# Expert weights loaded in rows of 16 KB, with the other tenants of the store packed into few pages

## The chip, the cores and the metric

The kernel runs on one core of one Trainium2 chip. The metric is the device time of one execution, in microseconds (us); lower is better. The kernel before takes 1248.84 us, the median of three executions (1247.45 to 1250.5).

## The reference, cut to what matters

One encoder layer on 512 tokens of width 1024, all in float32: token mixing with eight latent-attention heads and four differential-attention heads, then a mixture of 16 SwiGLU experts, each of which takes the 64 tokens with the highest affinity for it. Of the bytes that the layer reads, the three weight arrays of the experts are nearly all: 16 x 1024 x 2048, twice, and 16 x 2048 x 1024, in float32, which is 384 MiB.

```python
def reference(x, c, positions, ...):
    c_act = jax.nn.silu(c)
    mod = jnp.einsum('bd,dn->bn', c_act, w_ada[l]) + b_ada[l]
    sh_a, sc_a, g_a, sh_f, sc_f, g_f = jnp.split(mod[:, None, :], 6, axis=-1)
    u = x * (1.0 + sc_a) + sh_a
    mix = attention_mixer(u, positions, rel_bias, w_in[l], ..., w_out[l], l)
    x = layer_norm(DEEPNORM_ALPHA * x + g_a * mix, ln1_g[l], ln1_b[l])
    u = x * (1.0 + sc_f) + sh_f
    ffn = expert_choice_ffn(u, w_router[l], w_gate[l], w_up[l], w_down[l])
    return layer_norm(DEEPNORM_ALPHA * x + g_f * ffn, ln2_g[l], ln2_b[l])

def expert_choice_ffn(u, w_router, w_gate, w_up, w_down):
    cap = CAPACITY_FACTOR * S // N_EXPERTS                      # 64
    aff = jax.nn.softmax(jnp.einsum('bsd,de->bse', u, w_router), axis=-1)
    g, idx = lax.top_k(jnp.swapaxes(aff, 1, 2), cap)
    xs = jax.vmap(lambda ub, ib: ub[ib])(u, idx)
    h = jax.nn.silu(jnp.einsum('becd,edf->becf', xs, w_gate)) * jnp.einsum('becd,edf->becf', xs, w_up)
    y = jnp.einsum('becf,efd->becd', h, w_down) * g[..., None]
    ...                                                         # the rows of y are added back to their tokens
```

## The kernel before

**Stages.** In a first stage the modulation vector (products of `wadaT` with c, on DVE) and the first input projection (`w_a`, on PE) are made while their weights arrive: for each of eight blocks, two loads of `wadaT` (L207, L208), one of `xT` (L253) and one of `w_a` (L254). Behind it, in the same queue, come a table for the position bias, written by one DMA from `f_d` to `bias_d` in DRAM and read back (L481, L532), and the weights of the second projection, `w_q` (L326). Then come 32 attention steps, s = 0 to 31, whose extra work is put at a step by `at(...)`; the mixed heads are kept as `MX`, the rows of `w_out` are loaded by `wo_load` and split in two parts by `wo_split`, and the four blocks of x itself, for the residual sum, are loaded by `x_load` (L788). Up to here the list scheduler of the language sets the order of the instructions on each engine. From `crit` on the order is that of the code: output projection, layer norm, router, top-64 by `DVE.max`, and then the experts.

**Experts.** They go in eight pairs, pr = 0 to 7, and the two experts of a pair share the 128 rows of the array (64 tokens each). `gather` makes the transposed tokens `xs` by matmuls with a one-hot matrix, a scale `Gc` and a shift `Bc` per column of the model width. `up` multiplies them with `w_gate`, then with `w_up`, in eight steps k of 128 model rows; `hidden_t` transposes the product; `down` multiplies with `w_down` in eight steps b of 256 rows. `scatter` adds the result to the tokens, one pair later.

**The store.** 24 pages of 8 KB per partition (`Pages`) hold everything large: the weights and the data of the attention, and later the expert weights. `get` returns a free page, or a part of one, with the one that has been free longest first; `put` gives it back. The list `stream` has every load of expert weights in the order of use; each is 1 MiB, 8 KB in each of 128 partitions, and fills a page. `prefetch` issues loads from it, in SP's queue, for as long as a page is free:

```python
            for k in range(KB):
                for e in range(2):
                    off = w.offset + ((2 * pr + e) * D + k * P) * FF
                    stream.append(((pr, nm, k, e), bass.AP(tensor=w.tensor, offset=off, ap=[[FF, P], [1, FF]])))
...
    def prefetch(keep=0):
        while stream and pages.free() > keep:
```

It is called once at step 29 of the attention (with 3 pages kept), once ahead of `crit` (with 2 kept), once ahead of the top-64, and then in `turn`, which gives back the two pages of a step k or b when its matmuls have been written down. A load into a page that was given back waits, in SP's queue, for the last matmul that reads it. The matmuls on the weights of `up` are L1365, those of `down` and most others go through the helper `mm` (L121), and the transposes of `hidden_t` are L1396, those of the router L948.

## Time and profile before

| what | value |
|---|---|
| median of three executions | 1248.84 us |
| the profiled execution | 1253.39 us |
| its span in the trace | 1251.6 us |
| PE busy | 1173.6 us (94%) |
| DVE busy | 373.0 us (30%) |
| ACT busy | 229.6 us (18%) |
| POOL busy | 34.0 us (3%) |
| moved by DMA | 456.03 MB, mean 364 GB/s |
| mean granted clock of TensorE | 0.986 |

The span runs from the first to the last record of the profiled execution, and 1.8 us of its time lie around it. The span is cut into 40 slices of 31.3 us where the page gives a rate in slices. The busy shares are means over stages that differ: the first 320 us are the attention and the router, the rest are the experts. PE's time of a matmul record is modelled to its end, and its weight loads (PEld) overlap with it. A row of a group gives the line, the engine, the operation, its tiles and shapes, the count; then the busy time and the mean time of one in ns; then the idle time ahead of it and what ended most of it.

### The profile page before, as it was taken

The numbers are of one execution on the slowest core, as the hardware profiler recorded it, in microseconds if no ns is written. First come the engines' busy times: TensorE is split into PE (matmuls) and PEld (weight loads), VectorE is DVE, ScalarE is ACT, GpSimd is POOL, SyncE is SP. The second block draws the span as 40 slices with busy tenths as digits, with TensorE's granted clock in tenths as the row PEclk, the third lists the DMA queues.
The fourth block names the chain that finished last, engine by engine and source line by source line (L and its number), as shares of the span: only waits on it lengthen the run. The fifth ranks groups of instructions, "written<-read, shape, count | busy, mean of one in ns | idle before, by whom it ended". The sixth has DMA issues, their size and how long they took to land.

```text
span 1251.6 us, 14038 instructions
## 1 busy us (share of the span) xinstructions
PE 1173.6 (94%) x5657; PEld 554.1 (44%) x5657; DVE 373.0 (30%) x827; ACT 229.6 (18%) x473; POOL 34.0 (3%) x31
## 2 busy tenths in 40 slices
PE   8999999998999999999998899789979997999897
PEld 4877677775434333433432243234323432433232
DVE  6868889866001111111020102011101110111016
ACT  3555885433010000000000000000000000001001
POOL 0000000000000410000000000000000000000003
PEclk8999999998999899999999999999999999999998
DMA  9872426588999999999999999999999999999993
GB/s 335 314 269 90 164 99 211 175 338 344 366 420 422 420 390 422 422 420 421 421 422 421 420 421 422 421 420 422 422 420 421 422 422 421 420 422 421 421 401 130
DMA packets 76360, 456.03 MB, mean 364 GB/s; under 512 B 8285, under 2 KB 8669, under 8 KB 28163
## 3 DMA queue, kind: packets, MB, share of 16 engines
q1 hardware_dynamic: 76002, 455.02, 89.8%
q8 instruction: 44, 0.72, 0.2%
q14 instruction: 24, 0.19, 0.0%
q10 hardware_dynamic: 290, 0.10, 0.0%
HBM read 452.98 MB, written 3.95 MB: 365 GB/s over the span
## 4 chain that ended last, share of the span: by engine, by line
DMA 43%; PE 31%; DVE 1%; issue 0%; POOL 0%; ACT 0%; POOLq 0%; SPq 0%; DVEq 0%; ACTq 0%
DMA pg<-in_w_up_dram 17%; PE bk L121 17%; DMA pg<-in_w_down_dram 14%; PE bk L1365 13%; DMA pg<-in_w_gate_dram 11%; PE bk L1242 1%; POOL pg L1494 0%; PE bk L1396 0%; DVE lst L1476 0%; PE bk L1289 0%; POOLq L1623 0%; PE bk L1314 0%; DVE mv L1477 0%; DVE pg L1433 0%; ACT aff L879 0%
## 5 line engine op out<-in xcount | busy, mean ns | idle before, releaser
L1365 PE MATMUL bk<-pg,xs 128*64 128x512 f32 x2048 | 475.8, 602 | 49.2 <-DMA pg<-in_w_up_dram 47.6
L121 PE MATMUL bk<-pg,pg 128*64 128x512 f32 (+3 forms) x2138 | 466.2, 479 | 11.8 <-ACT pg L136 3.7
L121 PEld LDWEIGHTS bk<-pg,pg 128*64 128x64 f32 (+1 forms) x2138 | 236.9, 158 | 191.1 <-issue 130.6
L1365 PEld LDWEIGHTS bk<-pg,xs 128*64 128x64 f32 x2048 | 146.7, 137 | 350.4 <-issue 247.9
L1390 DVE TENSOR_TENSOR pg<-pg,bk 128x512 f32<-128x512 f32 x32 | 22.0, 687 | 338.4 <-PE bk L1365 310.1
L143 ACT ACTIVATE pg<-bk 128x512 f32<-128x512 f32 (+1 forms) x97 | 55.0, 582 | 352.0 <-PE bk L1396 318.2
L1300 DVE TENSOR_TENSOR pg<-pg,bk 128x512 f32<-128x512 f32 x56 | 38.5, 687 | 125.8 <-PE bk L121 125.4
L1283 DVE TENSOR_SCALAR xs<-bk,Gc,Bc 128x128 f32<-128x128 f32 x32 | 13.1, 410 | 207.9 <-PE bk L121 207.9
L121 PEld LDWEIGHTS bk<-ohg,pg 128*128 128x128 f32 x512 | 59.7, 191 | 27.3 <-issue 27.3
L121 PE MATMUL bk<-ohg,pg 128*128 128x128 f32 x512 | 66.0, 282 | 0.5 <-DVE ohg L1271 0.5
L121 PE MATMUL bk<-pg,ohg 128*128 128x512 f32 x120 | 59.2, 617 | 0.2 <-DVE pg L1433 0.2
L1281 ACT ACTIVATE xs<-bk,Bc,Gc 128x128 f32<-128x128 f32 x32 | 14.6, 457 | 201.3 <-PE bk L121 201.3
L143 ACT ACTIVATE ohg<-bk 128x512 f32<-128x512 f32 x8 | 4.8, 597 | 241.9 <-PE bk L1289 241.9
L136 ACT ACTIVATE pg<-pg 128x512 fp32r<-128x512 f32 (+2 forms) x63 | 42.7, 708 | 33.5 <-DMA pg<-in_w_q_dram 10.0
L1049 DVE CUSTOM_DVE_ANT_0 pg<-pg,pg 128x1024 f32<-128x1024 f32 x32 | 38.7, 1219 | 3.1 <-DMA pg<-in_wadaT_dram 3.1
L121 PEld LDWEIGHTS bk<-pg,ohg 128*128 128x128 f32 x120 | 20.4, 189 | 38.2 <-issue 37.6
L236 DVE TENSOR_TENSOR pg<-pg,pg 128x512 fp32r<-128x512 f32 (+1 forms) x34 | 31.0, 920 | 11.5 <-ACT pg L136 11.4
L1433 DVE SCALAR_TENSOR_TENSOR pg<-bk,lst,pg 128x512 f32<-128x512 f32 x16 | 12.0, 751 | 74.5 <-PE bk L121 73.7
L1386 ACT ACTIVATE pg<-bk 128x512 f32<-128x512 f32 x32 | 18.8, 598 | 60.2 <-PE bk L1365 60.2
L1396 PEld LDWEIGHTS bk<-csb,pg 128*128 128x128 f32 x128 | 17.7, 207 | 26.5 <-DVE pg L1390 13.5
L1450 POOL TENSOR_TENSOR pg<-pg,pg 128x512 f32<-128x512 f32 x4 | 5.1, 1273 | 786.9 <-DMA pg<-in_w_down_dram 782.9
L567 ACT ACTIVATE pg<-pg,st 128x512 f32<-128x512 f32 x32 | 23.0, 720 | 11.8 <-DVE st L563 11.6
(223 smaller groups left out, 594.6 us busy)
## 6 DMA issues: line engine op xcount, KB each, us to landing
pg<-in_w_gate_dram SPq DMA_DIRECT2D x128, 1024.0 KB, 19.8
pg<-in_w_up_dram SPq DMA_DIRECT2D x128, 1024.0 KB, 19.8
pg<-in_w_down_dram SPq DMA_DIRECT2D x120, 1024.0 KB, 19.8
pg<-in_wadaT_dram SPq DMA_DIRECT2D x16, 1024.0 KB, 6.4
pg<-in_wadaT_dram SPq DMA_DIRECT2D x16, 512.0 KB, 8.1
pg<-in_w_down_dram SPq DMA_DIRECT2D x16, 512.0 KB, 11.0
pg<-bias_d SPq DMA_DIRECT2D x16, 256.0 KB, 4.5
pg<-in_w_out_dram SPq DMA_DIRECT2D x8, 512.0 KB, 3.5
```

What stands on the lines that cost most here:

```text
L121: PE.matmul(o, l, r, start=start, stop=stop)
L136: return ACT.activation(dst, src, AF.Copy, scale=scale)
L143: ACT.activation(dst, src, AF.Copy)
L236: lo_eng.tensor_tensor(lo, src, ff(hi), op=OP.subtract)
L567: ACT.activation(pm, pm, AF.Exp, scale=-1.0, bias=nm[:, m:m + 1], accum_out=ss[:, m:m + 1])
L1049: i = DVE.tensor_tensor_reduce(out=w2[:, j], in0=w2[:, j], in1=cs, scale=1.0, scalar=0.0, op0=OP.mult, op1=OP.add, accum_out=modr[:, n:n + 1])
L1281: ACT.activation(xs[:, k, :], src, AF.Identity, scale=Gc[:, k:k + 1], bias=Bc[:, k:k + 1])
L1300: DVE.tensor_add(acc[t][:, c], acc[t][:, c], bank)
L1365: PE.matmul(banks[c][r], xs[:, k, r], w[e][:, c * 512:(c + 1) * 512], start=k == 0, stop=k == 7)
L1386: ACT.activation(EP["HS"][:, c * 512:(c + 1) * 512], banks[c], AF.Silu)
L1390: DVE.tensor_tensor(s, s, U[c], op=OP.mult)
L1396: PE.transpose(G[c % 2][:, i * P:(i + 1) * P], sj[:, i // 2, i % 2, :], ident)
```

## The change

**Rows.** A load of `w_gate` or `w_up` now takes two neighbouring model rows into one partition, so its rows are 16 KB and one load of 2 MiB serves two steps k (`block`). `gather` takes every second column of x to match, and `Gc` and `Bc` are rearranged to match by small matmuls (`GBp`). `w_down` comes with four neighbouring rows to a partition, and `hidden_t` transposes with a step of four. In the last pair `w_down` is loaded by pieces of 8 KB and of two times 2 KB in a row.

**Sheets.** A load of 2 MiB goes into a sheet of 16 KB per partition. The store is opened as 12 pools of two pages; when the top two pages are free, `sheet` closes that pool and opens one sheet in its place, from the other side. The eight lowest pages (`LOW`) stay pages. A sheet is given back after its second step. Where no sheet is to be had, `prefetch` may load the two halves of a block into two low pages, with rows of 8 KB (`begun`); in the first pair's first two projections, `turn` also allows that (`REUSE`).

**The other tenants.** `get` now chooses low pages, or pages 12 to 16 (`MID`), from step 22 on (`LATE`), and at once for what stays long (`stay`). Two of the mixed heads share a page, the last four splits of `w_out` have pages reserved for them (`WOR`), x has pages 0 and 1, which nothing else may use, and the last rows are loaded into the page of the first ones. `prefetch` is called at steps 30 and 31 too, with 4 pages kept.

The core of the diff:

```diff
+LOW = 8
+LATE = 22
+MID = (12, 17)
+REUSE = "gu"
...
+    def __init__(self, tc, ctx, n, low):
+        self.tc, self.ctx, self.low = tc, ctx, low
...
+    def open(self, name, side):
+        pool = self.tc.tile_pool(name=name, bufs=1, side=side).__enter__()
+        self.ctx.callback(lambda: pool._released or pool.release())
+        return pool
...
-        for i, u in enumerate(self.used):
-            if u and self.kind[i] != kind:
+        for i, u in enumerate(self.used[:top]):
+            if i < first or u and self.kind[i] != kind:
                 continue
...
-                key = (age, u == 0) if old else (u == 0, age)
+                high = (0 if i < self.low else i) if stay else (0 if MID[0] <= i < MID[1] else 1 if i < self.low else i)
+                key = (age, u == 0) if old else (high, u == 0, age) if self.late or stay else (u == 0, age)
                 if best is None or key < best[0]:
...
+    def has_sheet(self):
+        n = len(self.used)
+        return any(not u for u, _, _ in self.sheets) or n > self.low and not self.used[n - 1] and not self.used[n - 2]
+    def sheet(self):
+        free = [x for x in self.sheets if not x[0]]
+        if free:
+            x = min(free, key=lambda x: x[1])
+        else:
+            for v in (self.used, self.stamp, self.t, self.kind):
+                del v[-2:]
+            self.pools.pop().release()
+            i = len(self.sheets)
+            x = [0, 0, self.open(f"sheet{i}", bass.Side.RIGHT if hasattr(bass.Side, "RIGHT") else "right")]
+            self.sheets.append(x)
+        i = next(j for j, y in enumerate(self.sheets) if y is x)
+        self.now += 1
+        x[0] = 1
+        return ("sheet", i), x[2].tile([P, 4096], F32, name=f"sh{i}_{self.now}", tag=f"sh{i}", bufs=1)
...
+        self.now += 1
+        if i == "sheet":
+            assert self.sheets[m][0]
+            self.sheets[m][:2] = [0, self.now]
+            return
         assert self.used[i] & m == m
...
-            h, pg = pages.get()
+            h, pg = pages.get(first=0, top=2)
             Zh.append(h)
...
+        for h in range(2):
+            for j in range(2):
+                for i, v in enumerate((Gc, Bc)):
+                    o = 64 + 8 * i + j
+                    mm(bank[64 * h:64 * h + 64, o:o + 7:2], ident[:, j:127 + j:2], v[:, h:h + 7:2], True, True)
+        copy(ACT, GBp.rearrange("p i k -> p (i k)"), bank[:, 64:80])
...
+    def block(w, ex, rows, b, n):
+        return bass.AP(tensor=w.tensor, offset=w.offset + (ex * rows + b * n * P) * (4096 // n), ap=[[4096, P], [1, 4096]])
...
-            for k in range(KB):
+            for k in range(KB // 2):
                 for e in range(2):
-                    off = w.offset + ((2 * pr + e) * D + k * P) * FF
-                    stream.append(((pr, nm, k, e), bass.AP(tensor=w.tensor, offset=off, ap=[[FF, P], [1, FF]])))
...
-                off = w_down.offset + ((2 * pr + e) * FF + b * 2 * P) * D
-                stream.append(((pr, "d", b, e), bass.AP(tensor=w_down.tensor, offset=off, ap=[[2 * D, P], [1, 2 * D]])))
+                    stream.append(((pr, nm, k, e), block(w, 2 * pr + e, D, k, 2)))
+        for b in range(4):
+            if pr < NP - 1:
+                for e in range(2):
+                    stream.append(((pr, "d", b, e), block(w_down, 2 * pr + e, FF, b, 4)))
+            else:
...
-    def prefetch(keep=0):
-        while stream and pages.free() > keep:
-            key, src = stream.pop()
-            n = math.prod(src.shape[1:])
-            h, pg = pages.get(n // 256)
-            SP.dma_start(pg.rearrange("p (j n) -> p j n", j=2) if len(src.shape) == 3 else pg, src)
-            loaded[key] = (h, pg)
+    begun = []
+    def prefetch(keep=0, low=0, spare=None):
+        while stream and (not keep or pages.free() - 2 * (not begun) >= keep):
+            key, src = stream[-1]
+            if not begun and pages.has_sheet() and not (low == 2 and pages.free(LOW)):
+                h, pg = pages.sheet()
+                if isinstance(src, list):
+                    for n, part in enumerate(src):
+                        o = n % 2 * 2048 + n // 2 * 1024
+                        dst = pg[:, o:o + 2048] if len(src) == 2 else pg[:, o:o + 1024].rearrange("p (j n) -> p j n", j=2)
+                        SP.dma_start(dst, part)
+                else:
+                    SP.dma_start(pg, src)
+                loaded[key] = ([[], [h]], [pg[:, :2048], pg[:, 2048:]])
+                stream.pop()
+            elif (begun or low) and pages.free(LOW) > (0 if spare is None or begun else spare + 1):
+                h, pg = pages.get(top=LOW)
+                SP.dma_start(pg, bass.AP(tensor=src.tensor, offset=src.offset + 2048 * len(begun), ap=[[4096, P], [1, 2048]]))
+                begun.append((h, pg))
+                if len(begun) == 2:
+                    loaded[key] = ([[x] for x, _ in begun], [x for _, x in begun])
+                    begun.clear()
+                    stream.pop()
+            else:
+                break
 
...
+    at(27, ga[7], lambda: put_all([MXh[k] for k in range(4, 8)] + [WOh[k] for k in range(4, 8)]),
+       lambda: WOR.extend(pages.get(8, F32R, stay=True) for _ in range(4)), wo_next(0, 1))
...
+        if s == LATE:
+            pages.late = True
         if s in EARLY:
             prefetch(EARLY[s])
+        if s >= 30:
+            prefetch(4)
...
-                mm(src, Z[t][:, k * P:(k + 1) * P], oh[:, t, :], t == 0, t == 3)
+                mm(src, Z[t][:, k // 2 * 256 + k % 2:k // 2 * 256 + 255 + k % 2:2], oh[:, t, :], t == 0, t == 3)
             if k % 2:
-                ACT.activation(xs[:, k, :], src, AF.Identity, scale=Gc[:, k:k + 1], bias=Bc[:, k:k + 1])
+                ACT.activation(xs[:, k, :], src, AF.Identity, scale=GBp[:, 0, k:k + 1], bias=GBp[:, 1, k:k + 1])
             else:
-                DVE.tensor_scalar(xs[:, k, :], src, Gc[:, k:k + 1], Bc[:, k:k + 1], op0=OP.mult, op1=OP.add)
+                DVE.tensor_scalar(xs[:, k, :], src, GBp[:, 0, k:k + 1], GBp[:, 1, k:k + 1], op0=OP.mult, op1=OP.add)
...
+        if pr == 0 and nm in REUSE and k < 6:
+            prefetch(0, 1, 1)
...
+        for k in range(KB):
+            if k % 2 == 0:
+                h, w = zip(*(loaded.pop((pr, nm, k // 2, e)) for e in range(2)))
             between(k)
             for c in range(4):
-                products(k, c, w)
-            turn(pr, nm, k, h)
-        if n < KB:
...
+                products(k, c, [x[k % 2] for x in w])
+                if k >= n:
+                    columns(c)
+            turn(pr, nm, k, h[0][k % 2] + h[1][k % 2])
...
-        sj = EP["HS"][:, c * 512:(c + 1) * 512].rearrange("p (b q j) -> p b j q", b=2, j=2)
+        sj = EP["HS"][:, c * 512:(c + 1) * 512].rearrange("p (q j) -> p j q", j=4)
         for i in range(4):
-            PE.transpose(G[c % 2][:, i * P:(i + 1) * P], sj[:, i // 2, i % 2, :], ident)
+            PE.transpose(G[c % 2][:, i * P:(i + 1) * P], sj[:, i, :], ident)
```

SP's instructions in the first stage, before. In a row stand the line, the transfer and the shape; a tile's name has its page (`pg13`) and then serial numbers, and x2 is two loads in a row. `f_d` is the position bias on its way to the table in DRAM.

```order
L207 DMA pg13_20_182<-in_wadaT_dram 128x1024
L208 DMA pg13_20_182<-in_wadaT_dram 128x1024
L253 DMA pg11_15_139<-in_xT_dram 128x512
L254 DMA pg14_21_185<-in_w_a_dram 128x1024
L469 DMA f_d_74<-pg0_1_78 4x1024
L207 DMA pg17_27_226<-in_wadaT_dram 128x1024
L208 DMA pg17_27_226<-in_wadaT_dram 128x1024
L253 DMA pg14_21_185<-in_xT_dram 128x512
L254 DMA pg18_28_229<-in_w_a_dram 128x1024
L207 DMA pg20_33_269<-in_wadaT_dram 128x1024
```

The four loads of x come 70 rows further down, behind the loads of the table:

```order
L532 ISA
L532 DMA pg14_21_185<-bias_d_75 128x512
L788 DMA pg21_202_3464<-in_x_dram 128x1024 x2
L788 DMA pg7_201_3461<-in_x_dram 128x1024 x2
L210 DMA pg5_229_3649<-in_wadaT_dram 128x2x1024
L766 DMA pg18_223_3601<-in_w_out_dram 128x1024
L766 DMA pg20_232_3665<-in_w_out_dram 128x1024
```

The same place of the first stage, of the change:

```order
L247 DMA pg15_20_215<-in_wadaT_dram 128x1024
L248 DMA pg15_20_215<-in_wadaT_dram 128x1024
L293 DMA pg13_15_172<-in_xT_dram 128x512
L294 DMA pg16_21_218<-in_w_a_dram 128x1024
L828 DMA pg0_203_3497<-in_x_dram 128x1024 x2
L828 DMA pg1_204_3500<-in_x_dram 128x1024 x2
L509 DMA f_d_107<-pg2_1_111 4x1024
L247 DMA pg19_27_259<-in_wadaT_dram 128x1024
L248 DMA pg19_27_259<-in_wadaT_dram 128x1024
L293 DMA pg16_21_218<-in_xT_dram 128x512
L294 DMA pg20_28_262<-in_w_a_dram 128x1024
L247 DMA pg22_33_302<-in_wadaT_dram 128x1024
```

The four loads of x now stand ahead of the write to `f_d`, two blocks of `wadaT` and `w_a`, and all that follows them in the queue.

SP's instructions where the store is filled for the first time and then used again, before (`pg11_364` is a page that the first expert step has given back):

```order
L995 DMA pg6_353_4567<-in_w_gate_dram 128x2048
L995 DMA pg8_354_4569<-in_w_gate_dram 128x2048
L995 DMA pg22_355_4571<-in_w_gate_dram 128x2048
L995 DMA pg20_356_4573<-in_w_up_dram 128x2048
L995 DMA pg23_357_4575<-in_w_up_dram 128x2048
L995 DMA pg2_358_4577<-in_w_up_dram 128x2048
L995 DMA pg14_359_4579<-in_w_up_dram 128x2048
L995 DMA pg0_360_4581<-in_w_up_dram 128x2048
L995 DMA pg13_361_4583<-in_w_up_dram 128x2048
L995 DMA pg11_364_4653<-in_w_up_dram 128x2048
L995 DMA pg1_365_4655<-in_w_up_dram 128x2048
L995 DMA pg12_368_4670<-in_w_up_dram 128x2048
```

The same place of the change (`sh` is a sheet, 4096 elements wide; the page loads are halves):

```order
L1061 DMA sh3_329_4346<-in_w_gate_dram 128x4096
L1066 DMA pg6_351_4618<-in_w_gate_dram 128x2048
L1066 DMA pg4_352_4620<-in_w_gate_dram 128x2048
L1066 DMA pg7_353_4622<-in_w_gate_dram 128x2048
L1061 DMA sh4_354_4628<-in_w_gate_dram 128x4096
L1061 DMA sh5_355_4634<-in_w_up_dram 128x4096
L1061 DMA sh6_356_4640<-in_w_up_dram 128x4096
L1061 DMA sh7_357_4646<-in_w_up_dram 128x4096
L1061 DMA sh0_360_4729<-in_w_up_dram 128x4096
L1061 DMA sh1_361_4731<-in_w_up_dram 128x4096
L1061 DMA sh2_364_4759<-in_w_up_dram 128x4096
L1061 DMA sh3_365_4761<-in_w_up_dram 128x4096
```

Ahead of the first loads into room that the experts give back there were 22 loads of 1 MiB; now there are eight of 2 MiB and six halves, and the room that is given back first is two sheets, where it was two pages.

## Rows read from the trace of the kernel before

**Rows 1.** The page: span, GB/s in 40 slices, instruction queue (packets, MB, share).

```profile
span 1251.6 us, 14038 instructions
...
GB/s 335 314 269 90 164 99 211 175 338 344 366 420 422 420 390 422 422 420 421 421 422 421 420 421 422 421 420 422 422 420 421 422 422 421 420 422 421 421 401 130
...
q8 instruction: 44, 0.72, 0.2%
```

**Rows 2.** Stretches: length, busy us PE, PEld, DVE, ACT, POOL, PEclk, DMA, GB/s.

```profile
280.00:290.00 10.00, 10.00 (x68) 8.07 (x67) 6.99 (x33) 3.04 (x9) 0.00 (x0) 1.00 0.65 252
290.00:300.00 10.00, 5.98 (x56) 3.90 (x55) 7.57 (x33) 5.07 (x13) 0.00 (x0) 0.93 0.84 338
...
310.00:320.00 10.00, 10.00 (x61) 5.36 (x61) 0.82 (x2) 0.91 (x2) 0.00 (x0) 1.00 0.71 279
360.00:600.00 240.00, 239.96 (x1114) 92.11 (x1112) 33.86 (x56) 15.01 (x27) 18.73 (x8) 0.99 1.01 417
600.00:1200.00 600.00, 549.46 (x2472) 207.85 (x2470) 68.62 (x116) 31.76 (x58) 0.00 (x0) 1.00 1.01 421
```

**Rows 3.** PE's costliest group from 600 to 1200 us.

```profile
L1365 PE MATMUL bk<-pg,xs 128*64 128x512 f32 x1280 | 302.8, 601 | 49.2 <-DMA pg<-in_w_up_dram 47.6 <-DMA pg<-in_w_gate_dram 1.6
```

**Rows 4.** DMA issues, 600 to 1200 us: count, KB, median us to landing.

```profile
pg<-in_w_gate_dram SPq DMA_DIRECT2D x80, 1024.0 KB, 19.8
```

**Rows 5.** SP's timeline, 190 to 420 us: start, length, line, transfer, count.

```profile
227.54 0.34 SPq L995 DMA_DIRECT2D pg<-in_w_gate_dram  x1
...
245.96 46.23 SPq L995 DMA_DIRECT2D pg<-in_w_gate_dram  x12
292.24 43.32 SPq L995 DMA_DIRECT2D pg<-in_w_up_dram  x16
```

**Rows 6.** What SP waited for, whole run: us, times, longest.

```profile
SPq L995 <- PE bk L1365: 126.4, 76, 17.0
```

**Rows 7.** DMA packets, 1205 to 1215 us.

```profile
DMA packets 1924, 3.86 MB, mean 386 GB/s; under 512 B 113, under 2 KB 113, under 8 KB 1901
```

**Rows 8.** DMA packets and issues, 20 to 40 us.

```profile
DMA packets 2519, 8.12 MB, mean 406 GB/s; under 512 B 284, under 2 KB 284, under 8 KB 2517
...
pg<-in_wadaT_dram SPq DMA_DIRECT2D x8, 512.0 KB, 9.1
pg<-in_w_a_dram SPq DMA_DIRECT2D x4, 512.0 KB, 8.7
pg<-in_xT_dram SPq DMA_DIRECT2D x4, 256.0 KB, 8.3
```

**Rows 9.** DMA issues of the whole run: the four loads of x.

```profile
pg<-in_x_dram SPq DMA_DIRECT2D x4, 512.0 KB, 3.9
```

**Rows 10.** SP's timeline, 40 to 100 us.

```profile
43.60 0.79 SPq L481 DMA_DIRECT2D bias_d<-f_d  x1
47.14 7.40 SPq L326 DMA_DIRECT2D pg<-in_w_q_dram  x1
...
57.91 2.09 SPq L326 DMA_DIRECT2D pg<-in_w_q_dram  x1
66.58 4.15 SPq L532 DMA_DIRECT2D pg<-bias_d  x6
```

**Rows 11.** What ACT waited for, 40 to 100 us.

```profile
ACT pg L136 <- DMA pg<-in_w_q_dram: 10.0, 5, 5.4
```

**Rows 12.** PE's timeline, 308 to 331 us: the first expert steps.

```profile
312.39 3.65 PE L1365 MATMUL bk<-pg,xs 128*64 128x512 f32 x16
315.98 1.16 PE L121 MATMUL bk<-ohg,pg 128*128 128x128 f32 x8
317.07 3.65 PE L1365 MATMUL bk<-pg,xs 128*64 128x512 f32 x16
```

**Rows 13.** Transposes by group, whole run.

```profile
L1396 PE MATMUL bk<-csb,pg 128*128 128x128 f32 x128 | 23.8, 308 | 0.0
L948 PE MATMUL bk<-csb,pg 128*128 128x128 f32 x128 | 19.3, 274 | 0.1
```

More of the change, by code (lines that the diff above doesn't have):

```diff
@@ L53 @@
 class Pages:
-    def __init__(self, pool, n):
-        self.pool = pool
+    def __init__(self, tc, ctx, n, low):
+        self.tc, self.ctx, self.low = tc, ctx, low
+        self.pools = [self.open(f"pages{i}", bass.Side.LEFT if hasattr(bass.Side, "LEFT") else "left") for i in range(n // 2)]
+        self.sheets = []
         self.t = [None] * n
@@ L95, in put, with free @@
                 self.stamp[i][k] = self.now
-    def free(self):
-        return sum(u == 0 for u in self.used)
+    def free(self, top=None):
+        return sum(u == 0 for u in self.used[:top])
 @with_exitstack
@@ L112, in encoder_layer @@
     BK = [psum.tile([P, 512], F32, name=f"bk{i}") for i in range(8)]
-    pages = Pages(pagep, NPAGES)
+    pages = Pages(tc, ctx, NPAGES, LOW)
     f_d = dram.tile([4, 1024], F32, name="f_d")
@@ L228, in mod_add, with split @@
             DVE.tensor_add(modc[:, a:b], modr[:, a:b], bcol[:, a:b])
-    def split(src, n, lo_eng, late=False):
-        h, pg = pages.get(n * 8 // 1024, F32R)
+    def split(src, n, lo_eng, late=False, page=None):
+        h, pg = page or pages.get(n * 8 // 1024, F32R)
         hi, lo = pg[:, :n], pg[:, n:2 * n]
@@ L775, in wo_split @@
         after(i, EP["soft"][0])
-        WOh[k], WO[k] = split(raw, 1024, DVE)
+        WOh[k], WO[k] = split(raw, 1024, DVE, page=WOR[k] if k < 4 else None)
         pages.put(hr)
@@ L804, in encoder_layer @@
     Gc, Bc = fixed.tile([P, 8], F32, name="Gc"), fixed.tile([P, 8], F32, name="Bc")
+    GBp = fixed.tile([P, 2, 8], F32, name="GBp")
     wrg = rowb[:, :256].rearrange("p (k e) -> p k e", k=KB)
@@ L1175, in encoder_layer @@
     w(0, 1)
-    prefetch(KEEP)
+    prefetch(KEEP, 1)
     none = lambda: None
@@ L1419, in down @@
     def down(pr, Y, between):
[L1420 to L1422 removed]
+        for b in range(4 if pr == NP - 1 else 8):
+            if pr == NP - 1:
+                h, ws = loaded.pop((pr, "d", b))
+            elif b % 2 == 0:
+                h, w = zip(*(loaded.pop((pr, "d", b // 2, e)) for e in range(2)))
+            if pr < NP - 1:
+                ws = [x[b % 2] for x in w]
+            for j in (2 * b, 2 * b + 1):
                 for c in range(2):
```

84 lines of the change are left out of this document (36 added, 48 removed).

## The prediction, made ahead of the result

> **What bounds the kernel now.** I read the page's rate of the DMA engines by slices first, then the stretches, then what each side waits for. From the eleventh slice on the engines move some 420 GB/s without a gap until the last two [rows 1]. In the stretch from 600 to 1200 us they are busy all the time at 421 GB/s, while PE is busy for 549 of 600 us [rows 2], and the 49 us that PE idles ahead of its largest group end with a weight load landing [rows 3]. One load takes 19.8 us from issue to landing [rows 4]; 1 MiB at 421 GB/s is 2.49 us, so eight are queued and the engines never want for work. From 360 to 600 us PE has no idle time, yet the engines run at 417 GB/s [rows 2]: PE lives on what was loaded ahead, and the stream still decides when the end comes. So the time is: when the weight stream begins to run without gaps, plus its bytes by its rate, plus a tail. Between 270 and 320 us there are still gaps: 252, 338 and 279 GB/s in three of its stretches [rows 2]. The last of them is a full store: 22 loads fit (24 pages less two with x), SP issues them from 227.5 us [rows 5], and then waits for PE to free a page, once for 17.0 us [rows 6].
>
> So three things count: the rate, the moment at which the first expert matmul frees room, and how much one release frees. PE, DVE and ACT count only ahead of that moment.
>
> **The change, part by part.** *Rows of 16 KB.* What does a packet of 16 KB take? Rows of 2 KB run at 386 GB/s [rows 7], that is 2048 x 16 / 386 = 84.9 ns a packet on each of 16 engines; rows of 8 KB at 421, or 311.3 ns [rows 2]. A line through both has 9.4 ns per packet and 37.73 ns per KB. It gives 160.4 ns at 4 KB; in the early loads, where 24 rows of 4 KB go with 8 of 2 KB per engine, it gives 405 GB/s, and 406 is measured [rows 8]. At 16 KB the line gives 613.2 ns, 427.5 GB/s. A load of 2 MiB then takes 8 x 613.2 = 4.906 us in place of 4.981, 0.076 less. SP's order has 179 such loads; the first eight only fill the store, and 171 come behind. Gain: 171 x 0.076 = 13.0 us. Bounds: nothing, if the row moves as two packets of 8 KB; 171 x 8 x (622.6 - 603.7) ns = 25.8 us, if the fixed part vanished. The instruction queue moved 0.72 MB in 44 packets, 16.4 KB each [rows 1], so packets of this size exist; I take 13.0.
>
> The Trainium skill (DMA: Bandwidth & Descriptors, "Measured") speaks against that: it gives 425 GB/s for one transfer of 16 MB, the best of its table. By it the gain is 171 x (4.981 - 4.934) = 8.0 us, and the sum below comes to +2.2 us. Its table has 341 GB/s at 1 MB, where this trace has 421, so its figures hold a start-up that eight queued loads hide here; I go by the line.
>
> *x loaded ahead.* Pages 0 and 1 are now kept for x, so nothing holds its four loads back, and they move from behind the bias loads to the middle of the first stage. At 406 GB/s, the rate there [rows 8], 4 x 512 KB [rows 9] take 5.2 us on the queue. Behind them stand half of the first projection's weights, the bias table's write and the w_q loads. That piece is late already: the bias write is issued at 43.6 us, the second w_q load behind it at 57.9, the first bias loads at 66.6 [rows 10], and ACT waits 10.0 us for w_q in it, 5.4 at once [rows 11]. So the 5.2 us should reach the attention steps and the first expert matmul. Bounds: nothing, if PE's backlog (the w_a work) covers it; 5.2. I take 5.2, by rows 11. Nothing comes back at x's old place, where DMA was not the limit.
>
> *Sheets.* The store still holds 22 MiB ahead of the experts: eight sheets and six low pages. A page came free after one k step, at 312.39 + 3.65 = 316.04 us; a sheet holds two k steps and comes free with the second, at 317.07 + 3.65 = 320.72 [rows 12]. The stream, which stands full, starts again 4.7 us later. Bounds: 0, if the low pages' half loads bridge it; 9.4, if the next pair is late by as much. I take 4.7. Once the stream runs, eight sheets are enough: PE holds two, six are queued or landed, 6 x 4.906 = 29 us ahead. Starting the sheets earlier in the attention steps gains nothing where the store is full by the time it is needed.
>
> *Strides.* The gather reads Z with a step of two elements as weights. Transposes of such a stride take 308 ns where plain ones take 274 [rows 13], and up to 1.1 us would lie ahead of the first release (32 records); pipelined, I take 0.3. The hidden transposes' step of four lies beside 49 us of PE's waiting; uncovered, at 34 ns each, they cost 4.4 us in all. The eight small matmuls and the copy for GBp stand in the attention steps, under 1 us; last_rows reuses a page free for long; the packed MX and w_out pages change no count of loads: nothing.
>
> *Sum:* -13.0 + 5.2 + 4.7 + 0.3 = -2.8 us. The profiled execution's 1253.39 us (its span and 1.8 around it) becomes 1250.6; the median of the runs, 1248.84, becomes **1246.0 us**.
>
> **The rivals.** *The early x loads cost nothing.* For it: PE is busy in all of the first stage and may sit on a backlog. Against: ACT's wait [rows 11]. Then -8.0: 1240.8 us.
>
> *Half of the fixed part stays.* Each packet keeps more than a line through two points shows, the gain is 6.5: +3.7, 1252.5 us. For it: 8 KB rows keep the engines busy already, and two points carry the line. Against: the third, at 4 KB.
>
> *The rows bring nothing (the other side).* The engines move 16 KB as two packets, or the port is full: gain 0, +10.2, 1259.0 us. It decides against the change as soon as a load gains less than 10.2 / 171 = 0.060 us, at a packet over 615.1 ns (426.2 GB/s). Against: the instruction packets [rows 1].
>
> *The store isn't full in time.* A sheet needs two neighbouring pages free, so its first loads come later than 227.5 us [rows 5]. 22 loads need 55 us; begun after 260 us, they are not in by 315, and each us beyond costs one: at 270, 10 of which the gap of 279 GB/s [rows 2] pays 3: +4, 1253 us.
>
> *The fixed part nearly vanishes:* -15.6, 1233 us.
>
> **How the numbers follow.** What a measurement of this kernel tells from no change is 0.2%, 2.5 us. Forecast 0.40, just past that line, so 0.24 faster and 0.16 same; x costs nothing 0.17, faster; half stays 0.18, of which 0.10 same and 0.08 slower; nothing 0.10 and late store 0.09, slower but for 0.03; fixed part vanishes 0.06. Faster 0.47, same 0.29, slower 0.24. The range reaches from 1239, below the x rival, to 1256, above half and late; it leaves out the vanished part (0.06), rows that bring nothing (0.10) and 0.03 of late stores. The forecast's own range, 1243 to 1249, covers its strides and half of the sheets' bounds.
>
> **What would show it.** Right: 427 GB/s from 600 to 1200 us, with packets of 16 KB at some 613 ns; first expert matmul near 317.6 us; the stream's restart some 10 us later than 316; PE's idle time ahead of the gate and up groups lower by about 13 us. Wrong: a rate of 421 to 425 (rows); a first expert matmul near 312 (x); a gap in the rate past 330 us (sheets, late store); PE waiting for nothing after 600 us, so that it has become the bound.

## The result, and the profile after

The change made the kernel slower. In the first comparison it took 1260.68 us where before took 1249.28: a ratio of 1.0085, 95% interval 1.0071 to 1.0100. Timed again it was 1256.76 against 1250.53: 1.0048, 1.0033 to 1.0063 (one more execution of the change, with a granted clock of 0.65 where the others have 0.97 to 0.98, took 1670.18 us and is left out of the median). The forecast was 1246.0 with a range from 1239 to 1256. Three traces of the change have spans of 1257.8, 1254.8 and 1257.3 us, two of before 1251.6 and 1247.0, so the traces have 7.3 us between their means, and it is these 7.3 that can be followed to their places.

The page of the change, the same parts as [rows 1]:

```profile
span 1257.8 us, 13717 instructions
...
GB/s 343 315 220 160 118 76 143 168 369 268 331 403 426 416 399 425 427 427 428 426 425 429 426 427 426 427 428 426 426 426 428 426 427 427 428 427 426 424 401 134
```

The rate of the late slices is what the line through the packets had given, 427 where before had 421. Of the early ones most are lower: 220, 118, 76 and 143 GB/s in the third and the fifth to seventh slice, 268 and 331 in the tenth and eleventh. The stretches, with the columns of [rows 2]:

```profile
290.00:300.00 10.00, 10.00 (x68) 8.11 (x68) 6.88 (x34) 2.29 (x8) 0.00 (x0) 1.00 0.19 76
...
320.00:330.00 10.00, 10.00 (x60) 5.70 (x61) 0.82 (x2) 0.91 (x2) 0.00 (x0) 1.00 0.67 283
330.00:340.00 10.00, 10.00 (x52) 4.30 (x50) 0.41 (x1) 0.46 (x1) 0.00 (x0) 1.00 0.78 303
...
360.00:600.00 240.00, 235.69 (x1092) 90.03 (x1088) 29.25 (x49) 13.81 (x25) 18.71 (x8) 0.99 1.00 420
600.00:1200.00 600.00, 557.55 (x2496) 214.73 (x2498) 70.79 (x120) 31.24 (x57) 0.00 (x0) 0.98 1.01 427
```

What DMA moved from 600 to 1200 us, of the change and then of before in its second trace:

```profile
DMA packets 17864, 255.96 MB, mean 427 GB/s; under 512 B 1983, under 2 KB 1983, under 8 KB 1983
```

```profile
DMA packets 34881, 252.69 MB, mean 421 GB/s; under 512 B 3861, under 2 KB 3861, under 8 KB 4121
```

That is 1.3% more, and PE's idle time ahead of the same group as in [rows 3] fell from 49.2 us to 41.6:

```profile
L1447 PE MATMUL bk<-sh,xs 128*64 128x512 f32 x1304 | 308.9, 616 | 41.6 <-DMA sh<-in_w_up_dram 41.6
```

So the late part is faster, by about as much as the whole kernel is slower. PE's timeline at the first expert steps answers to [rows 12]:

```profile
322.82 3.65 PE L1447 MATMUL bk<-sh,xs 128*64 128x512 f32 x16
326.41 1.21 PE L161 MATMUL bk<-ohg,pg 128*128 128x128 f32 x8
327.55 3.65 PE L1447 MATMUL bk<-sh,xs 128*64 128x512 f32 x16
331.13 1.21 PE L161 MATMUL bk<-ohg,pg 128*128 128x128 f32 x8
```

And SP's timeline shows the loads that waited for them:

```profile
331.23 10.25 SPq L1061 DMA_DIRECT2D sh<-in_w_up_dram  x4
345.40 0.91 SPq L1066 DMA_DIRECT2D pg<-in_w_up_dram  x2
358.53 0.33 SPq L1061 DMA_DIRECT2D sh<-in_w_down_dram  x1
```

The first expert matmul comes 10.4 us later than in the trace shown of before, and the first load into released room is issued 8.4 us behind it, with the end of the second step (327.55 + 3.65 = 331.20), as the prediction had it.

**Where the 7.3 us are.** The packet records of the traces tell when how many bytes were still to come, in us from the start of the span; each row is a mean over three traces of the change and two of before:

| place (MB of all that DMA moves) | before, us | change, us | difference grows by |
|---|---|---|---|
| first expert matmul | 311.6 | 321.8 | +10.2 |
| 380 MB still to come | 323.0 | 337.8 | +4.6 |
| 370 MB still to come | 347.2 | 363.9 | +1.9 |
| 320 MB still to come | 467.3 | 483.6 | -0.4 |
| 250 MB still to come | 633.4 | 647.5 | -2.2 |
| 5 MB still to come | 1216.2 | 1223.0 | -7.3 |
| end of the span | 1249.3 | 1256.6 | +0.5 |

The restart in the first pair costs 4.6 and then 1.9 us, up to 320 MB next to nothing comes back, and from there on the change gains 9.5 us at an even pace. Two stretches on either side of that place, of the change and then of before in its second trace:

```profile
420.00:480.00 60.00, 60.00 (x248) 20.39 (x246) 8.70 (x14) 4.30 (x8) 18.71 (x8) 0.97 0.99 406
480.00:600.00 120.00, 115.71 (x542) 43.73 (x538) 13.58 (x23) 6.01 (x11) 0.00 (x0) 1.00 1.01 427
```

```profile
420.00:480.00 60.00, 60.00 (x253) 20.08 (x253) 6.51 (x11) 3.58 (x6) 18.71 (x8) 0.97 1.01 420
480.00:600.00 120.00, 119.26 (x564) 45.84 (x560) 18.24 (x30) 7.20 (x13) 0.00 (x0) 1.00 1.01 421
```

From 420 to 480 us SP waits for PE to give back room and the change falls to 406 GB/s, for the last time ahead of the last pieces. Behind 480 us it runs at 427 where before has 421, although PE is still busy for 115.71 of the next 120 us.

### The profile page after: what moved, and what is told of

Same layout as the page of the kernel before. It is cut to its first block, busy times and chain, and to the rows that moved or that the text cites. A ratio compares the mean times of both kernels' runs of the same rounds, so it can differ in the third digit from the quotient of the medians.

```text
span 1257.8 us, 13717 instructions
## 1 busy us (share of the span) xinstructions
PE 1175.4 (93%) x5673; PEld 560.6 (45%) x5673; DVE 373.6 (30%) x827; ACT 229.0 (18%) x474; POOL 34.0 (3%) x31
## 4 chain that ended last, share of the span: by engine, by line
PE 54%; DMA 19%; DVE 2%; issue 0%; POOL 0%; ACT 0%; POOLq 0%; SPq 0%; ACTq 0%; DVEq 0%
PE bk L161 28%; PE bk L1447 24%; DMA sh<-in_w_up_dram 14%; DMA sh<-in_w_down_dram 5%; PE bk L1472 1%; PE bk L1371 0%; DVE small L1321 0%; DVE ohg L1323 0%; POOL pg L1577 0%; DVE lst L1559 0%; POOLq L1706 0%; DVE pg L1516 0%; SPq L1061 0%; PE bk L1396 0%; DVE mv L1560 0%
## 5 line engine op out<-in xcount | busy, mean ns | idle before, releaser
L1447 PE MATMUL bk<-sh,xs 128*64 128x512 f32 x1984 | 469.4, 610 | 45.4 <-DMA sh<-in_w_up_dram 45.4
L1447 PEld LDWEIGHTS bk<-sh,xs 128*64 128x64 f32 x1984 | 146.8, 140 | 336.6 <-issue 263.4
L161 PE MATMUL bk<-pg,pg 128*128 128x512 f32 (+3 forms) x1132 | 234.4, 374 | 18.7 <-ACT pg L176 4.9
L161 PE MATMUL bk<-sh,pg 128*64 128x512 f32 x1008 | 235.9, 597 | 1.4 <-DMA sh<-in_w_down_dram 1.4
L161 PEld LDWEIGHTS bk<-pg,pg 128*128 128x128 f32 (+1 forms) x1132 | 168.3, 180 | 66.9 <-issue 12.2
L161 PEld LDWEIGHTS bk<-sh,pg 128*64 128x64 f32 x1008 | 70.5, 136 | 131.3 <-issue 120.1
L1365 DVE TENSOR_SCALAR xs<-bk,GBp 128x128 f32<-128x128 f32 x32 | 13.1, 409 | 210.8 <-PE bk L161 210.8
L161 PEld LDWEIGHTS bk<-ohg,pg 128*128 128x128 f32 x512 | 62.9, 196 | 27.3 <-issue 27.3
L161 PE MATMUL bk<-ohg,pg 128*128 128x128 f32 x512 | 69.3, 288 | 0.5 <-DVE ohg L1353 0.5
L1363 ACT ACTIVATE xs<-bk,GBp 128x128 f32<-128x128 f32 x32 | 14.6, 458 | 203.7 <-PE bk L161 203.7
L1126 DVE CUSTOM_DVE_ANT_0 pg<-pg,pg 128x1024 f32<-128x1024 f32 x32 | 38.7, 1219 | 2.7 <-DMA pg<-in_wadaT_dram 2.7
```

Of the source, the lines that this page charges most:

```text
L161: PE.matmul(o, l, r, start=start, stop=stop)
L1126: i = DVE.tensor_tensor_reduce(out=w2[:, j], in0=w2[:, j], in1=cs, scale=1.0, scalar=0.0, op0=OP.mult, op1=OP.add, accum_out=modr[:, n:n + 1])
L1363: ACT.activation(xs[:, k, :], src, AF.Identity, scale=GBp[:, 0, k:k + 1], bias=GBp[:, 1, k:k + 1])
L1365: DVE.tensor_scalar(xs[:, k, :], src, GBp[:, 0, k:k + 1], GBp[:, 1, k:k + 1], op0=OP.mult, op1=OP.add)
L1447: PE.matmul(banks[c][r], xs[:, k, r], w[e][:, c * 512:(c + 1) * 512], start=k == 0, stop=k == 7)
```

## The experiments

All but two runs were timed beside before, whose median was 1250.1 to 1250.5 us each time.

**x loaded late, and x loaded early alone.** The first is the change with the order of before for x:

```diff
-        SP.dma_start(bt, bass.AP(tensor=bias_d.tensor, ...
+        EP["bl"] = SP.dma_start(bt, bass.AP(tensor=bias_d.tensor, ...
-                SP.dma_start(z, x[t * P:(t + 1) * P, :])
+                after(SP.dma_start(z, x[t * P:(t + 1) * P, :]), EP["bl"])
```

> The change with one thing undone: the four loads of x stand behind the last load of the bias table in SP's queue, as before; their pages stay reserved. In the change the first expert matmul began at 322.8 us where it began at 312.4 before. Theory A: the early loads cause all of that, 10.4 us where the prediction had 5.2. Then the first expert matmul begins near 312.5 us, ACT waits some 10 us for w_q in the stretch from 40 to 130 us (18.2 in the change), and the time is near 1250 us. Theory B: they cost 5.2 us, and the rest comes from the new choice of pages in the attention steps. Then 317.6 us and a time near 1255.5. Theory C: they cost nothing: 322.8 us and 1260.7.

The second is before, with pages 0 and 1 kept for x as in the change:

```diff
-        for i, u in enumerate(self.used):
-            if u and self.kind[i] != kind:
+        for i, u in enumerate(self.used[:top]):
+            if i < first or u and self.kind[i] != kind:
...
-            h, pg = pages.get()
+            h, pg = pages.get(first=0, top=2)
```

> The kernel before with one part of the change alone: pages 0 and 1 kept for x, and its four loads ahead of the write of the bias. Rows, sheets and the rest are those of before. Theory A: the first expert matmul moves from 312.4 to some 322.8 us and the time from 1249.3 to 1259.5. Theory B: 317.6 us and 1254.5. Theory C: no difference, 1249.3.

Measured: the change with x late took 1254.62 us (1.0043, 1.0025 to 1.0060), before with x early 1256.36 (1.0057, 1.0037 to 1.0077). Their first expert matmuls began at 316.02 and 317.04 us. ACT's wait for `w_q` from 40 to 130 us, of the change, of the change with x late, and of before with x early:

```profile
ACT pg L176 <- DMA pg<-in_w_q_dram: 18.2, 4, 10.8
```

```profile
ACT pg L176 <- DMA pg<-in_w_q_dram: 11.6, 4, 5.2
```

```profile
ACT pg L136 <- DMA pg<-in_w_q_dram: 16.1, 4, 10.4
```

Theory B holds: at the first expert matmul x early costs 5.8 us in the change (its mean, 321.8, less 316.02) and 5.4 in before (317.04 less its mean, 311.6), by the wait that the prediction named. In the time it costs 6.0 us in before; in the change 1.9 or 7.1, by which of its two comparisons is taken. It leaves 4.4 us of the 10.2 unexplained.

**Rows of 8 KB in the sheets.**

```diff
-                    SP.dma_start(pg, src)
+                    for n in range(2):
+                        SP.dma_start(pg[:, 2048 * n:2048 * (n + 1)],
+                                     bass.AP(tensor=src.tensor, offset=src.offset + 2048 * n, ap=[[4096, P], [1, 2048]]))
```

> The change with one thing undone: every load of a whole sheet is issued as two loads of 1 MiB, one for each half of the sheet, with rows of 8 KB; sheets, order, pages and releases stay. Theory R (the rows alone raise the rate): 421 GB/s from 600 to 1200 us where the change has 427, packets of some 311 ns, and a time 10.5 us above the change (what the stream won back behind its start), near 1271 us. Rival S (the rate comes from loads of 2 MiB or from fewer waits in SP's queue, not from the rows): 424 to 427 GB/s and 1261 to 1266 us.

Measured: 1270.93 us (1.0159, 1.0132 to 1.0186) and 251.74 MB from 600 to 1200 us. Theory R, as far as the edit goes: the sheets, their order and their releases stay, so they don't make the rate. But the edit halves the load together with its rows, and no run has loads of 2 MiB with rows of 8 KB. For the rows speak the packet records: two packets of 8 KB took 630.1 ns here, one of 16 KB takes 616.9 in the change (means from 620 to 1190 us). And 251.74 is less than the 252.69 of before, so part of the 10 us belongs to something else; it is found below.

**No sheets; no sheets and no rules.** Both have x late. The first loads every block by halves into two pages, the second also takes pages as before:

```diff
+            h, pg = pages.get()
+            SP.dma_start(pg, bass.AP(tensor=src.tensor, offset=src.offset + 2048 * n, ap=[[4096, P], [1, 2048]]))
...
-LATE = 22
+LATE = 99
-                key = (age, u == 0) if old else (high, u == 0, age) if self.late or stay else (u == 0, age)
+                key = (age, u == 0) if old else (high, u == 0, age) if self.late else (u == 0, age)
```

> The first experiment (the change with x loaded late) without sheets: every block comes as two loads of 1 MiB with rows of 8 KB into two pages, wherever one is free, and each page is given back after its own step. The rules for the choice of pages in the attention steps, the packed mixed rows, the reserved w_out pages and the strides stay. In the first experiment the first expert matmul began at 316.0 us, 3.6 later than before, with PE waiting more between 100 and 250 us. Theory P: the rules of page choice cost these 3.6 us, and the release by whole sheets costs 4.7 more behind it and the missing gain of the rows is 10.3. Then the first expert matmul begins near 316.0, the first load into a page given back is released 3.7 us behind it, and the time is 1250.3 + 3.6 = 1254 us. Rival Q1: the sheets themselves, begun in SP's queue in the attention steps, hold up other loads there. Then 312.4 us and 1250.3.

> The same without the rules of page choice too: get takes the page that has been free longest, as before (pages 0 and 1 stay kept for x). Left of the change are the packed mixed rows, the reserved w_out pages, the strides of gather and hidden_t, GBp, and the calls of prefetch at steps 30 and 31. Theory P: the first expert matmul is back near 312.4 us and the time at that of before, 1250.3. Rival Q2 (what is left costs it): 316.0 us and 1254.

Measured: 1263.83 us with the rules (1.0104, 1.0089 to 1.0119), 1258.83 without (1.0060, 1.0048 to 1.0072); first expert matmul at 317.24 and 313.44 us. So the rules of page choice cost 3.8 us ahead of the experts and 5.0 in the time, as theory P has it. But its times, 1254 and 1250.3, are both missed, by 9.8 and 8.5 us. Stretches of the version with the rules:

```profile
280.00:290.00 10.00, 10.00 (x88) 7.67 (x87) 6.45 (x29) 2.27 (x7) 0.00 (x0) 1.00 0.03 12
290.00:300.00 10.00, 9.62 (x79) 7.29 (x77) 8.19 (x33) 2.75 (x8) 0.00 (x0) 1.00 0.18 50
...
320.00:330.00 10.00, 10.00 (x54) 4.17 (x50) 0.41 (x1) 0.46 (x1) 0.00 (x0) 1.00 1.01 417
```

The engines stand nearly still up to 300 us and then run at their full rate past the first release at 320.9 us (317.24 + 3.65). So the store wasn't full when the first page came back, an earlier release could win nothing, and this version doesn't show what the sheets cost. What the rules do is seen in what SP waited for from 185 to 265 us, in the change and in before:

```profile
SPq L250 <- DVE modr L1126: 20.6, 4, 13.3
SPq L250 <- PE bk L161: 17.9, 3, 10.9
SPq L250 <- DMA pg<-in_wadaT_dram: 10.0, 4, 4.8
```

```profile
SPq L210 <- DVE modr L1049: 16.1, 2, 14.5
```

With few pages to choose from, a load of `wadaT` (L250) is put into the page that the last one still uses, waits for its product (L1126), and keeps all that stands behind it in SP's queue. PE then waits once, from 185 to 265 us, for DVE's product in `q_proj` (L787), which goes into a page that `get` has just given: in the change, in the version without sheets and with rules, and not in the one without rules:

```profile
PE bk L161 <- DVE pg L787: 3.1, 1, 3.1
```

```profile
PE bk L161 <- DVE pg L787: 2.5, 1, 2.5
```

```profile
PE bk L161 <- DVE pg L276: 0.3, 1, 0.3
```

That this one wait, of 2.5 to 3.1 us, is most of the 3.8 is argued from its size, not shown.

**Sheets later.** The attention of the last version, the store filled by 22 pages, and sheets only from pages that the experts have given back (a table `ORDER` numbers the pages so that neighbours come free together):

```diff
+ORDER = [0, 1, 9, 8, 11, 17, 18, 7, 12, 23, 22, 4, 20, 16, 13, 6, 10, 19, 14, 2, 15, 5, 21, 3]
-        for i, u in enumerate(self.used[:top]):
+        for i in ORDER:
...
-            prefetch(EARLY[s])
+            fill_store(EARLY[s])
```

> Rows of 16 KB without what the other experiments found them to cost: x late, no rules of page choice, the store filled for the first time by loads of 1 MiB into 22 pages in the order in which the attention gives them back; the numbering of the pages is such that the first six loaded are the low ones and the others lie in pairs from the top, so that a pair becomes a sheet when its second step is over. The low pages are loaded again after the first two steps. Theory P: first expert matmul near 312.4 us, the next loads released 3.7 us behind it, 427 GB/s from 600 to 1200 us, and 1250.3 - 10.3, up to 2.5 more for two low pages that are no longer loaded: 1240 to 1243 us. Rival: most of the gain of the rows is only what the change had lost at its start (a stream that lags has more to win back while PE is behind); then 1246 to 1250.

> As the version with sheets made later (1251.6 us), but the pages are numbered so that the two pages that one and the same step gives back are neighbours: a sheet can be loaded after each of the first seven steps and the ninth, and no step waits for a second one. There the rate from 310 to 340 us was 220, 276 and 228 GB/s, where before had 320, 378 and 426 in its second trace: some 9.8 us of loading lost. Theory P (what one release frees decides the start of the stream): these come back, the stretch runs as before, and the time is 1241 to 1244 us, the first version faster than before. Rival: the room is lost later in the first pair, when the low pages go to other tenants: 1247 to 1252.

Measured: 1251.58 us (1.0013, 1.0004 to 1.0022) and 1251.74 (1.0013, 1.0002 to 1.0024): both missed theory P, and the second is what its rival said. The first expert matmul was early enough (311.14 and 313.47 us) and 426 GB/s were there behind 600 us. The first lost loading where two steps must end before room is free, the second, which repaired that, lost it 80 us later. Stretches of the first, then of the second:

```profile
310.00:320.00 10.00, 10.00 (x55) 4.71 (x54) 0.41 (x1) 0.91 (x2) 0.00 (x0) 1.00 0.60 220
320.00:330.00 10.00, 10.00 (x54) 4.62 (x52) 0.41 (x1) 0.46 (x1) 0.00 (x0) 1.00 0.69 276
330.00:340.00 10.00, 10.00 (x51) 3.90 (x52) 0.41 (x1) 0.46 (x1) 0.00 (x0) 1.00 0.66 228
```

```profile
410.00:420.00 10.00, 10.00 (x48) 3.34 (x48) 1.50 (x2) 0.46 (x1) 0.00 (x0) 1.00 0.62 229
```

PE is busy all of that time: it is behind, the store is full, and room for a load comes only as fast as PE gives it. As long as that holds, a faster load only fills the store sooner.

**Sheets from a later pair on.** Then nothing should be lost: before as it is for the first pairs, the change's rows, sheets, strides and `GBp` for the rest, `Q` = 2 (from the third pair on) or 3.

```diff
+        if pr >= Q:
+            n = KB if columns is None else KB - 1
+            for k in range(KB):
+                if k % 2 == 0:
...
+            if key[0] < Q:
+                h, pg = pages.get()
+                SP.dma_start(pg, src)
+            else:
+                h, pg = pages.sheet()
```

> The kernel before, with its attention, its choice of pages, its order and its rows for the first two pairs of experts; from the third pair on rows of 16 KB, sheets and strides as in the change. The pages are numbered so that each step of the second pair's last projection gives back two neighbours, which become a sheet at once. Theory P (the rows gain 1.3% of the rate wherever the store isn't full, and cost nothing where they come late): 426 to 427 GB/s from 600 to 1200 us, 256.1 MB there, and 1250.3 - 8 = 1241 to 1244 us. Rival: a lower mean clock of PE (0.98 there with sheets, 1.00 before) or another wait takes it back: 1247 to 1251.

> The same with rows of 16 KB from the fourth pair on, so 5 pairs in place of 6. PE stops being the one that is late near 600 us, which is about where the loads of the fourth pair begin. Theory P: each pair of 120 us gains 1.3%, 1.6 us, so this one is 1.6 us slower than the one from the third pair on, 1242 to 1245 us. If the store is still full in the third pair, this one is the faster of the two.

Measured: 1245.02 us from the third pair (0.9963, 0.9949 to 0.9977) and 1247.20 from the fourth (0.9970, 0.9958 to 0.9982), with 255.58 MB from 600 to 1200 us in the first. These are the first versions faster than before, by 5.5 and 3.3 us. Theory P is right in kind; the two are 1.0 and 2.2 us above their forecasts, and what the lower clock of PE (0.98 as in the change) costs isn't shown.

The second expectation had a condition: with the store still full in the third pair, the later start would be the faster one. It is the slower one, by 2.2 us of medians whose intervals overlap, and the traces show the place. From 310 to 250 MB still to come, where the loads of the third pair run, the version from the third pair on takes 141.0 us, the one from the fourth 142.9, before 142.5 and 142.5. The same stretch of both:

```profile
480.00:600.00 120.00, 119.62 (x558) 46.25 (x556) 18.22 (x30) 7.21 (x13) 0.00 (x0) 1.00 1.01 426
```

```profile
480.00:600.00 120.00, 119.97 (x567) 46.26 (x564) 18.22 (x30) 7.20 (x13) 0.00 (x0) 1.00 1.01 420
```

PE has no idle time to speak of in either. So a faster row gains as soon as the store is no longer full, even while PE is still busy all the time.

**The order of the loads.** The version without sheets and rules is 8.5 us behind before with its first expert matmul only 1.9 behind the mean of before. The next version has the loads, gather and transposes of before, and a second one has their order too (the two experts alternate):

```diff
-                SP.dma_start(pg, bass.AP(tensor=src.tensor, offset=src.offset + 2048 * n, ap=[[4096, P], [1, 2048]]))
+                SP.dma_start(pg, bass.AP(tensor=src.tensor, offset=src.offset + 2048 * P * n, ap=[[2048, P], [1, 2048]]))
...
+            key, src = stream[-1 - n % 2] if two else stream[-1]
```

> The last of the three without rules took 1258.8 us, 8.5 above before, though its first expert matmul began at 313.4 us, one later than before: 420 GB/s from 600 to 1200 us, and the end of the stream further behind. Here the loads, gather, scales and transposes are those of before (a load is 1 MiB in a row in DRAM, 8 KB in each partition, no strides); left are the packed mixed rows, the reserved pages for w_out and x, the calls at steps 30 and 31 and the shared page for the last rows. Theory T: rows of 8 KB that lie 16 KB apart in DRAM are slower than rows that follow each other, and the strides and the order of the halves cost the rest. Then 421 GB/s and 1250 to 1252 us. Rival U (the packing and the reserved pages cost it): 1256 to 1259.

> The version with the loads of before in all but their order (1257.3 us, 6.9 above before): there a block's two loads from one expert's matrix follow each other, 2 MiB in a row, and then come those of the other expert; here the two experts alternate with every load of 1 MiB, as before. From 600 to 1200 us that version moved 251.73 MB, before 252.74 and 252.75. Theory O (the order is the cause, by the rate and by a step that has to wait for the third load of a block): 252.7 MB and 1250 to 1252 us. Rival U (the pools of two pages, the packing or the reserved pages): 251.7 MB and 1256 to 1258.

Measured: 1257.27 us (1.0052, 1.0037 to 1.0067) and 1257.92 (1.0057, 1.0042 to 1.0072), 251.77 and 251.78 MB. Theories T and O are both wrong: neither the pitch in DRAM nor the order moves the time by more than the 1.6 us that lie between these two and the version without sheets and rules.

**64 bytes.** Among what these versions share with the change and not with before is `GBp`, 64 bytes ahead of the pages.

```diff
+    pad = fixed.tile([P, 16], F32, name="pad")
+    DVE.memset(pad, 0.0)
```

> The kernel before with one unused tile of 64 bytes in the fixed part, so that its pages begin at byte 32736 of a partition in place of 32672, where those of the change begin. Theory L (the place of the pages sets the time of a packet): 315.04 ns and 251.7 MB from 600 to 1200 us, and 1250.5 + 2.5 = 1253 us. Rival (something else that the five share): 314.15 ns, 252.7 MB and 1250.5.

> The kernel before with its small tiles put together, so that the pages begin at byte 32576, a multiple of 64, where 32672 and 32736 are 32 more than one. Theory L says only that the packets take another time; if multiples of 64 matter, a shorter one than 314.15 ns, and 1 to 3 us less than 1250.5. Rival: 314.15 ns and 1250.5.

> The kernel with rows of 16 KB from the third pair on (1245.0 us), with its pages at byte 32672 as before in place of 32736. Theory L: its packets of 16 KB take 1 to 2 ns less than 616.98, the rate from 600 to 1200 us passes 427 GB/s, and the time is 2 us less, 1243. Rival: the same as there, 1245.

Measured: before with its pages 64 bytes up took 1253.89 us (1.0032, 1.0020 to 1.0045), 96 bytes down 1250.99 (1.0006, 0.9996 to 1.0015), and the fast version with its pages where before has them 1245.00 (0.9958, 0.9942 to 0.9973), no other time than at 64 bytes up. DMA from 600 to 1200 us with the pages 64 bytes up, and 96 bytes down:

```profile
DMA packets 34555, 251.79 MB, mean 420 GB/s; under 512 B 3840, under 2 KB 3840, under 8 KB 3840
```

```profile
DMA packets 34728, 252.65 MB, mean 421 GB/s; under 512 B 3851, under 2 KB 3851, under 8 KB 3926
```

Theory L holds for packets of 8 KB. For those of 16 KB it isn't tested: the sheets are opened from the other end of the store, so they lie at the same bytes in both fast versions (98272 and up, in steps of 16384), and moving the pages leaves them there. Their packets took 616.9 ns on average in both, and the equal times say nothing against theory L. The 96 bytes down shorten a packet from 314.15 to 313.93 ns, and no gain in time is seen.

The 64 bytes explain some 4 of the 7 us of the last two versions (2.5 to 5.6 by the interval); the rest is open. Their traces have some 2 to 3 us of it behind the last 5 MB of the stream, where they issue the last pieces in another way.

**Second traces.** Before and the change once more, one run each with a trace.

> The kernel before once more, with a profile: its profiled execution took 1253.39 us where the runs shown had a median of 1249 and a range from 1245 to 1253. If the trace of before was at the slow end by a late start of the experts, the first expert matmul begins near 308 us here; if by the rate, it stays near 312.4 and the stretch from 600 to 1200 us has more than 421 GB/s.

> The change once more with a trace. By the differences so far its first expert matmul begins near 322.8 us again, and the rate from 600 to 1200 us is 427 GB/s; if the early x loads move other things from run to run, it is elsewhere by more than 2 us.

Measured: 1248.81 and 1256.58 us; the first expert matmul at 310.76 and 320.85 us, with 252.69 and 255.93 MB from 600 to 1200 us. The place of before, 310.76, is neither of the two that were expected. So single traces differ by 2 us ahead of the experts, and the late rate doesn't vary. The change once more with timing is the second ratio at the head of this part.

> The change once more, timed beside the others on one chip: 1260.7 in its four runs, while its two traces are 1259.6 and 1256.6 and those of before 1253.4 and 1248.8. If the traces are a fair sample the difference is near 7 us (1257.5), if the timed runs are, near 11 (1261).

It came out at 1256.76 us, 6.2 above before and close to where the traces put it. Why the first comparison has 5 us more isn't settled; no trace shows them.

## Why the prediction was wrong

**What bounds the kernel: right, but from a later moment on.** The sentence "when the weight stream begins to run without gaps, plus its bytes by its rate, plus a tail" holds from some 480 us on. Ahead of that the change's store is full at the restart and again from 420 to 480 us; there the stream's rate is that of the room PE gives back, and a faster row only fills the store sooner.

**Rows of 16 KB, -13.0: right in mechanism, mis-sized: -9.5.** The rate came as forecast (427), and the experiment with 8 KB puts it down to the rows, or to the size of a load that came with them. The Trainium skill (DMA: Bandwidth & Descriptors, "Measured") has 425 GB/s for 16 MB, the best of its table; this trace has 427, so the measurement decides. From 320 to 5 MB still to come the change needs 739.4 us in each of three traces, before 748.8 and 749.1, a gain of 1.3% where the line had 1.5%. These 315 MB are as much as 150 loads of 2 MiB, so a load gained 0.063 us where the line had 0.076. Two things failed: at 0.063 the 171 loads are 10.8 us, 2.2 less than forecast, and the count "171 come behind" takes in loads ahead of 480 us, whose gain was lost again in waiting for room, 1.3 us more.

**x loaded ahead, +5.2: right.** 5.8 us in the traces of the change, 6.0 in the time for it alone.

**Sheets, +4.7: right in mechanism, +6.1 with what followed.** The stream restarted with the end of the second step, and fell 4.6 us further behind up to 380 MB; 1.9 came on top up to 370 MB, and 0.4 came back up to 320. From its first expert matmul to 380 MB the change needs 16.0 us, before 11.2 and 11.5, and before with x early, which has no sheets, 11.2. No run takes the sheets alone out of the change and keeps its store full, so the share of other parts isn't shown.

**Strides, +0.3: not shown apart.** The gather's eight matmuls take 1.21 us where they took 1.16 [rows 12].

**The step that failed most: the rules of page choice have no term in the sum.** The nearest sentences are "the packed MX and w_out pages change no count of loads: nothing", and "Starting the sheets earlier in the attention steps gains nothing". I looked at what these edits move in the stream and not at what they take from others: fewer pages to choose from in the attention steps, so that loads wait in SP's queue for pages still in use. With and without the rules the first expert matmul differs by 3.8 us and the time by 5.0; in the change x leaves 4.4 us for them. The packing and the reserved pages are in both of these versions, and without the rules the first expert matmul is 1.9 us behind the mean of before, no more than single traces differ. The order of SP's loads could have told it: before, the last ten loads of `wadaT` go to seven pages, in the change seven of the ten go to two, and without the rules they go to seven again.

With these, 5.8 + 4.4 + 6.1 - 9.5 + 0.5 = 7.3 us, the last term behind the end of the stream. Of the prediction's signs the rate of 427 came; the packets took 616.9 ns in place of 613, the first expert matmul was at 321.8 us in place of 317.6, and PE's idle time fell by 7.6 us in place of 13. The rival that gave nearly the measured time, rows that bring nothing (1259.0), is wrong in its mechanism, and its nearness is luck. The sign turned because a loss counted as nothing, 4.4 us, and a gain counted 3.5 us too high make up 8 of the 10 us between -2.8 and 7.3.

## What to carry to other kernels

A faster transfer gains only from the moment on at which the buffers are full for the last time: look for that moment, and count the gain behind it. It can lie well ahead of the first wait of the consumer; here it was near 480 us, and PE first waited near 580. A rule that keeps buffers free for one stage is paid in the stage that loses them, so look in the queue's order at which loads now share a buffer. Where a new layout costs at a start, it can be begun in the middle of the run: from the third pair on, the same rows made the kernel 0.4% faster.

## What the runs showed of the hardware

The place of a buffer in the partition changes the time of a packet: with the pages beginning at byte 32736 instead of 32672, packets of 8 KB took 315.04 ns on average in place of 314.15 (mean of the packet records from 620 to 1190 us, the same within 0.04 ns in every one of the traces with each place), and the kernel 0.32% longer. At byte 32576 they took 313.93 ns, in one trace. Packets of 16 KB took 616.9 ns; the runs have them at one set of places only. Why is open.
